# A hybrid diffusion step: the first feed-forward without Strassen products, squares summed by TensorE, and GpSimd kept off VectorE's work during normalisations

## The chip, the core and the metric

The kernel runs on one core of one Trainium2 chip. The metric is the device time of one execution in microseconds (us). Shown before the change: 2499.05 us, the median of 3 runs (2495.54 to 2499.7).

The core's engines are named as in the profile: PE is TensorE (matrix products, into the banks of PSUM), PEld its loading of stationary operands, DVE is VectorE, ACT is ScalarE, POOL is GpSimd, and SP is SyncE, which starts the transfers. Each engine runs its own stream of instructions in order.

## The reference

One step of a two-layer model over 128 context tokens and 512 latent tokens of width 1024. Each layer is a half-step SwiGLU feed-forward (FFN), a token mixer, and a second FFN. Layer 0 mixes by two attentions side by side (A, grouped-query with a band, and B, multi-head latent attention), layer 1 by a two-dimensional Fourier transform.

```python
def post_norm(x, out, gate, g, b):
    return layer_norm(ALPHA * x + gate[:, None, :] * out, g, b)
...
def half_ffn(x, shift, scale, gate, w_gate, w_up, w_down, g, b):
    h = modulate(x, shift, scale)
    return post_norm(x, FFN_HALF * swiglu(h, w_gate, w_up, w_down), gate, g, b)
...
    for l in range(DEPTH):
        mc = ada_mods(c_ctx[None, :], w_ada[l], b_ada[l])
        ms = ada_mods(c, w_ada[l], b_ada[l])
...
        y_s = half_ffn(y_s, ms[0], ms[1], ms[2], *ffn_pre)
        h_p = modulate(y_p, mc[3], mc[4])
...
        y_s = post_norm(y_s, o_s, ms[5], ln_g[l, 1], ln_b[l, 1])
...
        y_s = half_ffn(y_s, ms[6], ms[7], ms[8], *ffn_post)
```

All arithmetic is float32, and `modulate` is x * (1 + scale) + shift. The nine modulations of each layer (numbers 0 to 8: shift, scale and gate, three times) are matrix-vector products with a 1024 x 9216 matrix.

## The kernel before, in words

**Layout.** Features lie on the 128 partitions (eight tiles of them, `KT`), tokens along the free dimension. The 640 tokens are split in two halves, 256 and 384 columns at first and 254 and 386 later, so that one half's normalisation can run while TensorE works on the other half.

**Products.** A float32 product is made of three products of a high and a low part (`mm3`: hi*hi, hi*lo, lo*hi), so each weight and each activation is split first: a cast gives the high part (`hh`, `hd`, `wu`, `w`), a subtraction the low part (`hl`, and again `hd`, `wu`, `w`).

**The feed-forwards.** `ffn` lists units and runs them in order. The hidden width of 2816 is 22 blocks `f`. A "gk" unit (a head) and a "g" unit make the gate and up products of a block for one half, plain: 96 matmuls for a block, 48 on each half's columns. An "s" unit makes both for all tokens by a Strassen form: seven products of half-size operands, 84 matmuls of 320 columns for a block. Its operands are sums and differences of quarters of the activations (`form`, tiles `tmp` and `xt`, once for an FFN) and of the weights (`weights`, once for a block), and its seven results are added up by further VectorE instructions. `seven=(6, 17)` says which blocks are "s" units. The down products ("d" units) run by groups of blocks: `THREES` has eight groups, `FOURS` has six. Each "d" output is added to the residual `ya` with the gate (`ya<-a,gate,ya`). The first group's down products are called D0 below.

**The modulations.** `matvec` is one VectorE instruction over 128x1024 (it writes the tile `junk`, two instructions for each 512 KB load of `w_ada`). `ffn` spreads `ada` such loads over its length, the first `urgent` of them early. `ada_beside(16)` spawns 16 more beside the attention mixer.

**Normalisation.** `norm_sum` adds the eight tiles of `ya` as they come; `norm` has TensorE turn that sum into a mean on all partitions, subtracts it (`centre`), squares (`square`), adds the eight squares up in one tile `lns`, and calls `rstd`: a one-column matmul for each 128 columns (`psc<-ones,lns`) sums over the partitions, small VectorE instructions make the inverse root, and a matmul with a diagonal (`psc<-dg,ones`) brings it to all partitions. `apply` scales, and `h_split` makes the operands of the next products. The half that the next stage needs first is the held half (`self.hold`). A path with `delta`, used after the Fourier mixer and at the very end, sums squares another way.

**Who does what, in what order.** The class `Step` writes the program as a planner: each task is a generator, and it names the engines that could do its next instruction with an estimated duration for each. `choose` takes the engine that would start and end it first by the modelled clock; between VectorE ("v") and GpSimd ("g") that is

```python
        e = min(on, key=lambda e: max(now, starts[e]) + on[e] + SPARED * (e == "v"))
```

so that an addition goes to GpSimd when VectorE's modelled queue is long. The order on each engine is fixed by this when the program is built.

Of the kernel before, what the change touches and what calls it, by code (L numbers as in the profile page):

```python
# [19 lines left out]
D = 1024  # L20
# [262 lines left out]
class Step:  # L283
# [7 lines left out]
    def __init__(self, ctx, tc, io):  # L291
# [9 lines left out]
        self.side, self.begun, self.hold, self.order = [], 0, 0, ORDER  # L301
        self.const = self.pool(ctx, "const")
# [90 lines left out]
    def choose(self, on, what):  # L393
# [6 lines left out]
        now = self.nc.tensor.t if self.clock.fixed > 100 else 0  # L400
        e = min(on, key=lambda e: max(now, starts[e]) + on[e] + SPARED * (e == "v"))
# [165 lines left out]
    def rstd(self, q, n, eps, out, delta=None, banks=None):  # L567
# [4 lines left out]
        width = q.shape[1]  # L572
        k = -(-width // 128)
        if delta is None:
            yield "t", q
        yield "t", lambda: banks.free(1) and self.smalls.free(1) and self.diags.free(1)
        col, t, dg = banks.take(), self.smalls.take(), self.diags.take()[:, :width]
        v, hv, y = t[:, 0, :k], t[:, 1, :k], t[:, 4, :k]

        cs = [min(i * 128, width - 128) for i in range(k)]  # L580
# [14 lines left out]
        for i, c in enumerate(cs):  # L595
            self.mm(col[:, i:i + 1], q[:, c:c + 128], self.ones[:, 0:1], start=True, stop=True)
        self.sums.give(q)
# [147 lines left out]
    def square(self, half, st, o, n):  # L745

        ya = self.ya[half]
        if o:
            yield None, lambda: self.tmps.free(1)
        eng = yield {"s": 93 + 0.833 * n, **sums(n)}, ya[o]  # L750
        if o:
            yield None, lambda: self.tmps.free(1)
        sq = self.tmps.take()[:, :n] if o else st["q"]
# [4 lines left out]
        if o == 5 and "d" not in st:  # L758
# [12 lines left out]
    def norm(self, half, st, i, aff, ag, plain=False, spill=None, kept=True):  # L771
# [4 lines left out]
        self.hold += held  # L776
        delta = st.get("d")
# [8 lines left out]
        if delta is None:  # L786
            self.sums.give(s)
            yield "v", lambda: self.sums.free(1)
            st.update(q=self.sums.take()[:, :n], squares=0)
# [15 lines left out]
        q = st["q"]  # L805
# [6 lines left out]
        yield from self.rstd(q, D, LN_EPS, bc, delta, banks)  # L812
# [12 lines left out]
        def apply(o):  # L825
# [3 lines left out]
            if not left[0]:  # L829
                banks.give(bc)  # L830
                self.hold -= held
            if aff is None:
# [32 lines left out]
    def start(self, ops):  # L865
# [6 lines left out]
        raws, owner = {}, {}  # L872

        def load(o):
            for m in (1, 0):

                sl = owner[o, m] = self.xt if len(raws) % 2 else ops
                raws[o, m] = sl.take(dtype=F32)[:, :D]
# [18 lines left out]
        def weighed(o):  # L897
# [4 lines left out]
            owner[o, 1].give(raws[o, 1])  # L902
            known[o] += 1

        def scale(o):
# [5 lines left out]
            owner[o, 1].give(raws[o, 1])  # L911
# [5 lines left out]
        def shift(o):  # L917
# [3 lines left out]
            owner[o, 0].give(raws[o, 0])  # L921
            known[o] += 1

        def part(half, o):
# [4 lines left out]
            yield None, lambda: self.xroom(o)  # L929
            eng = yield scaled(self.n[half], len(self.segs[half])), sh  # L930
            yield None, lambda: self.xroom(o)
            t = self.xplace(half, o)
            self.modulated(eng, half, z, (s1, sh), o, t)
            self.spawn(alpha(z), "g", z)
            yield from self.h_split(half, o, t, self.h, False)
# [1664 lines left out]
```

## Time and profile before

| | |
|---|---|
| median of 3 runs | 2499.05 us |
| the profiled execution's own time | 2503.09 us |
| its span, first to last instruction | 2501.3 us |
| mean granted TensorE clock | 0.961 |
| PE busy | 2356.0 us (94%), 15113 instructions |
| DVE busy | 2011.3 us (80%), 4099 |
| ACT busy | 948.5 us (38%), 2071 |
| POOL busy | 574.2 us (23%), 557 |
| read from HBM | 247.79 MB, 101 GB/s over the span |

The profiled execution is one single run, and rows of the trace belong to it. Its span runs from the first to the last instruction; the 1.8 us between span and time lie around it. Busy time is the time in which an engine had an instruction under way. The granted clock is the share of full speed that TensorE was given, 1.00 being 2.4 GHz and 0.50 being 1.2 GHz.

The stages, by the tiles that the trace names: first FFN to 510 us, attention mixer to 880, its output product and normalisation to 930, second FFN of layer 0 to 1398, first FFN of layer 1 to 1880, Fourier mixer to 2036, last FFN to 2478, last normalisation to the end.

### The profile page before, as it was taken

The page shows a single profiled execution, that of the slowest core. Times are in us where ns is not written, and L with a number is a line of the kernel's source. Part 1 is how long each engine was busy: PE and PEld are TensorE (multiplying, and loading weights), DVE is VectorE, ACT ScalarE, POOL GpSimd, SP SyncE. Part 2 cuts the span into 40 slices and gives each one's busy share as a digit, 9 for nine tenths or more (in the row PEclk, how much of TensorE's full clock was granted, in tenths as well). Part 3 has the DMA queues.
Part 4 walks back from the last instruction along what each step waited for, and adds up shares of the span by engine and source line. Part 5 has one row for each costly group of instructions (what it writes and reads, how often), then busy time and mean ns, then how long its engine had stood idle before and what let it go on. Part 6 is the DMA issues. An engine that isn't in the chain of part 4 may idle for free. (4 is left out here: it accounts for less than half of the span.)

```text
span 2501.3 us, 40294 instructions
## 1 busy us (share of the span) xinstructions
PE 2356.0 (94%) x15113; PEld 2248.9 (90%) x15113; DVE 2011.3 (80%) x4099; ACT 948.5 (38%) x2071; POOL 574.2 (23%) x557
## 2 busy tenths in 40 slices
PE   7999999989989998999999899999996999999996
PEld 6999999978568898999999889999995788999996
DVE  7868999689667778688995887989969798777766
ACT  3323442253556634233331432434225344444332
POOL 7301011052322333011110530002116452000001
PEclk7999999999799998999999899999998999999998
DMA  6433335233122212333352043434524211222211
GB/s 247 140 96 115 119 127 196 91 109 96 30 63 66 78 62 81 118 118 122 124 167 87 18 131 97 127 127 132 164 86 153 93 51 44 88 88 86 85 60 43
DMA packets 98562, 258.02 MB, mean 103 GB/s; under 512 B 15224, under 2 KB 28216, under 8 KB 98368
## 3 DMA queue, kind: packets, MB, share of 16 engines
q1 hardware_dynamic: 98368, 255.45, 31.7%
q8 instruction: 119, 1.95, 0.3%
q14 instruction: 75, 0.61, 0.1%
HBM read 247.79 MB, written 5.52 MB: 101 GB/s over the span
## 5 line engine op out<-in xcount | busy, mean ns | idle before, releaser
L463 PE MATMUL a<-hh,wu 128*128 128x254 f32 (+4 forms) x2856 | 689.2, 315 | 13.4 <-POOL wu L200 7.8
L463 PEld LDWEIGHTS a<-hh,wu 128*128 128x128 f32 x2856 | 501.4, 192 | 15.7 <-POOL wu L200 8.1
L463 PE MATMUL a<-hd,wu 128*128 128x386 f32 (+3 forms) x2736 | 460.4, 313 | 16.9 <-ACT tmp L200 5.8
L463 PEld LDWEIGHTS a<-hd,wu 128*128 128x128 f32 x2736 | 420.2, 192 | 20.5 <-ACT tmp L200 6.0
L463 PE MATMUL a<-hl,wu 128*128 128x320 f32 (+4 forms) x1356 | 426.0, 314 | 8.6 <-POOL hl L200 7.7
L200 ACT CAST wu<-raw 128x512 fp32r<-128x512 f32 (+1 forms) x422 | 276.6, 676 | 398.3 <-DMA raw<-in_w_gu 126.8
L200 DVE CUSTOM_DVE_ANT_0 junk<-raw,cond,bada 128x1024 bf16<-128x1024 f32 x256 | 353.6, 1381 | 21.5 <-DMA raw<-in_w_ada 19.0
L200 DVE SCALAR_TENSOR_TENSOR ya<-a,gate,ya 128x128 f32<-128x128 f32 (+3 forms) x768 | 297.5, 433 | 70.7 <-PE a L463 67.7
L200 DVE TENSOR_TENSOR wu<-raw,wu 128x512 fp32r<-128x512 f32 (+1 forms) x362 | 285.2, 799 | 40.4 <-ACT wu L200 36.0
L463 PE MATMUL a<-hh,w 128*128 128x320 f32 (+6 forms) x1192 | 311.2, 317 | 2.1 <-ACT hh L200 2.1
L463 PE MATMUL a<-xt,wu 128*128 128x320 f32 (+2 forms) x1868 | 294.2, 310 | 4.2 <-ACT tmp L200 4.2
L463 PEld LDWEIGHTS a<-xt,wu 128*128 128x128 f32 x1868 | 277.5, 188 | 7.5 <-ACT tmp L200 5.9
L463 PEld LDWEIGHTS a<-hl,wu 128*128 128x128 f32 x1356 | 260.5, 192 | 10.9 <-POOL hl L200 8.5
L200 POOL TENSOR_TENSOR wu<-raw,wu 128x512 fp32r<-128x512 f32 (+1 forms) x57 | 97.1, 1708 | 584.6 <-ACT wu L200 511.7
L463 PE MATMUL a<-hd,w 128*128 128x386 f32 (+3 forms) x1200 | 223.3, 313 | 4.3 <-POOL hd L200 1.7
L463 PEld LDWEIGHTS a<-hh,w 128*128 128x128 f32 (+1 forms) x1192 | 212.6, 190 | 5.8 <-ACT hh L200 3.5
L463 PE MATMUL a<-hl,w 128*128 128x320 f32 (+6 forms) x668 | 211.1, 316 | 1.2 <-POOL hl L200 1.1
L463 PEld LDWEIGHTS a<-hd,w 128*128 128x128 f32 x1200 | 188.4, 190 | 6.6 <-POOL hd L200 2.2
L200 ACT CAST w<-raw 128x512 fp32r<-128x512 f32 (+3 forms) x189 | 122.6, 659 | 188.6 <-DVE raw L200 67.8
L200 ACT CAST hd<-tmp 128x320 fp32r<-128x320 f32 (+4 forms) x176 | 79.1, 459 | 227.3 <-DVE tmp L200 185.4
L200 POOL TENSOR_TENSOR w<-raw,w 128x512 fp32r<-128x512 f32 (+3 forms) x44 | 64.9, 1478 | 423.4 <-ACT w L200 382.0
L200 DVE TENSOR_TENSOR tmp<-tmp,a 128x320 f32<-128x320 f32 (+4 forms) x126 | 61.0, 484 | 95.9 <-PE a L463 89.2
(441 smaller groups left out, 3489.2 us busy)
## 6 DMA issues: line engine op xcount, KB each, us to landing
raw<-in_w_gu SPq DMA_DIRECT2D x176, 512.0 KB, 4.2
raw<-in_w_ada SPq DMA_DIRECT2D x128, 512.0 KB, 3.7
raw<-in_w_dn SPq DMA_DIRECT2D x176, 256.0 KB, 2.9
raw<-in_w_fin SPq DMA_DIRECT2D x16, 520.0 KB, 5.0
raw<-in_w_ab SPq DMA_DIRECT2D x11, 512.0 KB, 4.7
xt<-in_w_ada SPq DMA_DIRECT2D x8, 512.0 KB, 7.5
raw<-in_w_abo SPq DMA_DIRECT2D x8, 512.0 KB, 4.1
raw<-in_w_fout SPq DMA_DIRECT2D x8, 512.0 KB, 3.7
```

Source lines behind the costliest of these rows:

```text
L200: return getattr(self.engine, op)(*args, **kw)
L463: pe.engine.matmul(out, w, x, **kw)
```

## The change

Six things change:

1. The first FFN is plain throughout (`seven=None`), with the six groups of `FOURS`; it has 18 work slots where it had 10 and another pool beside them.
2. A counter `norming` is up while any normalisation runs. While it is up, `choose` doesn't give GpSimd anything that VectorE could do.
3. In the half that is not held, and without `delta`, each squared tile goes to TensorE, which sums it by one-column matmuls that accumulate in a bank (`st["col"]`), in place of additions into one tile.
4. The 16 loads and 32 matrix-vector instructions beside the attention mixer are gone. The first FFN has 8 loads more (48), the second 8 more, early ones (40, of them 8 urgent).
5. In the FFNs with no urgent modulations, D0 stood right behind the heads; now it stands behind the next plain or Strassen block, as in the first FFN.
6. Loads for the next stage, issued at an FFN's end, are no longer held back during a held half's normalisation.

```diff
+        if self.norming and "v" in on:
+            on = {e: on[e] for e in on if e != "g"}
         e = min(on, key=lambda e: max(now, starts[e]) + on[e] + SPARED * (e == "v"))
...
-        for i, c in enumerate(cs):
+        for i, c in enumerate(() if summed else cs):
             self.mm(col[:, i:i + 1], q[:, c:c + 128], self.ones[:, 0:1], start=True, stop=True)
...
+        if "col" in st:
+            yield "t", sq
+
+            for i, c in enumerate(cs := self.blocks(n)):
+                self.mm(st["col"][:, i:i + 1], sq[:, c:c + 128], self.ones[:, 0:1],
+                        start=not st["squares"] and not i, stop=st["squares"] == KT - 1 and i == len(cs) - 1)
+            self.tmps.give(sq)
+        elif o == 5 and "d" not in st:
...
+            if held:
+                yield "v", lambda: self.sums.free(1)
+                st.update(q=self.sums.take()[:, :n], squares=0)
+            else:
+
+                yield "t", lambda: banks.free(1)
+                st.update(col=banks.take(), squares=0)
...
-            if g == last or g == 1 and not urgent:
+            if g == last:
                 units, held = units + held, []
...
-                self.load_in(*e[2:4], 0 if e[4:] and e[4] < urgent else -1)
+                self.ada_live += e[4:] not in ((), (None,))
+                self.load_in(*e[2:4], 0 if e[4:] and (e[4] is None or e[4] < urgent) else -1)
...
-                ops = self.work_slots(pool, 10, True)
+                ops = self.work_slots(pool, 18, True)
...
-                self.ffn(0, 0, 0, (0, 3), pool, ops, {}, 0, THREES, 40, 8, after, True, spill=saved, kept=False)
+                self.ffn(0, 0, 0, (0, 3), pool, ops, {}, 0, FOURS, 48, 8, after, True, seven=None, spill=saved, kept=False)
...
-            self.spawn(self.ada_beside(16), first=-2)
...
-                self.ffn(0, 1, 2, (1, 0), pool, ops, old, 5, THREES, 32, 0, self.first_blocks(1, 0, got, ops, 2, is_w))
+                self.ffn(0, 1, 2, (1, 0), pool, ops, old, 5, THREES, 40, 8, self.first_blocks(1, 0, got, ops, 2, is_w))
```

Counted in the two programs: the first FFN loses 924 matmuls of 320 columns and gains 528 of 384 and 528 of 256. The summing of squares uses 42 one-column matmuls more (three normalisations with 16 in place of 2). GpSimd's stream falls from 545 to 452 instructions.

**Squares, between the FFNs of layers 0 and 1.** On TensorE, before the change, the squares of the 254-column half are one tile `lns` that two one-column matmuls sum (the other names are the products of the half that came first, with `hh` and `hl` its high and low parts):

```order
L463 MATMUL a_14634<-hh_85,w_14242 128x386
L463 MATMUL a_14635<-hh_85,w_14244 128x386
L463 MATMUL a_14635<-hl_93,w_14244 128x386
L463 MATMUL a_14635<-hh_85,w_14245 128x386
L463 MATMUL psc_14795<-ones,lns_14735 128x1 x2
L463 MATMUL a_14761<-hh_78,wu_14716 128x386
L463 MATMUL a_14761<-hl_86,wu_14716 128x386
```

With the change, at the same place, each squared tile `tmp` has its own pair; four pairs stand here, and the other four follow at once:

```order
L468 MATMUL a_14381<-hh_84,w_13995 128x386
L468 MATMUL psc_14467<-ones,tmp_14481 128x1 x2
L468 MATMUL psc_14467<-ones,tmp_14490 128x1 x2
L468 MATMUL a_14380<-hh_85,w_13991 128x386
L468 MATMUL a_14380<-hl_93,w_13991 128x386
L468 MATMUL a_14380<-hh_85,w_13992 128x386
L468 MATMUL a_14381<-hh_85,w_13994 128x386
L468 MATMUL a_14381<-hl_93,w_13994 128x386
L468 MATMUL a_14381<-hh_85,w_13995 128x386
L468 MATMUL psc_14467<-ones,tmp_14507 128x1 x2
L468 MATMUL psc_14467<-ones,tmp_14510 128x1 x2
```

The two matmuls with `lns` became eight pairs with `tmp`, spread between the products of the 386-column half; the squares come from ScalarE here, and no addition of squares is left.

**D0 in the first FFN of layer 1.** On TensorE, before the change, the last head's products (`hh_85` with `wu`) are followed at once by D0 (`hd`):

```order
L463 MATMUL a_15174<-hh_85,wu_14816 128x254
L463 MATMUL a_15174<-hl_93,wu_14816 128x254
L463 MATMUL a_15174<-hh_85,wu_14837 128x254
L463 MATMUL a_15249<-hd_14792,wu_14886 128x254
L463 MATMUL a_15249<-hd_14793,wu_14886 128x254
L463 MATMUL a_15249<-hd_14792,wu_14886 128x254
```

With the change another block's products follow the heads:

```order
L468 MATMUL a_14930<-hh_85,wu_14604 128x254
L468 MATMUL a_14930<-hl_93,wu_14604 128x254
L468 MATMUL a_14930<-hh_85,wu_14676 128x254
L468 MATMUL a_15005<-hh_78,wu_14724 128x386
L468 MATMUL a_15005<-hl_86,wu_14724 128x386
L468 MATMUL a_15005<-hh_78,wu_14738 128x386
```

and D0 comes 96 matmuls later, behind the last of that block:

```order
L468 MATMUL a_15102<-hh_85,w_14845 128x254
L468 MATMUL a_15102<-hl_93,w_14845 128x254
L468 MATMUL a_15102<-hh_85,w_14866 128x254
L468 MATMUL a_15134<-hd_14552,w_14870 128x254
L468 MATMUL a_15134<-hd_14553,w_14870 128x254
L468 MATMUL a_15134<-hd_14552,w_14870 128x254
```

Between the last head and D0 a whole block now stands, on both halves.

**GpSimd at the start of the second FFN of layer 0.** Before the change, the 386-column half's operands (`xt`, `hl`), a weight's low part (`wu`) and the residual's scaling (`ya`):

```order
L200 TENSOR_SCALAR xt_9630<-ya_0_9167,affa,affb 128x386
L200 TENSOR_SCALAR xt_9644<-ya_2_9169,affa,affb 128x386
L200 TENSOR_TENSOR hl_87<-xt_9630,hh_79 128x386
L200 TENSOR_SCALAR xt_9674<-ya_4_9171,affa,affb 128x386
L200 TENSOR_SCALAR xt_9674<-ya_5_9172,affa,affb 128x386
L200 TENSOR_TENSOR wu_10044<-raw_9835,wu_9837 128x1024
L200 TENSOR_SCALAR ya_1_9168<-ya_1_9168,ag 128x386
L200 TENSOR_SCALAR ya_4_9171<-ya_4_9171,ag 128x386
L200 TENSOR_TENSOR tmp_10038<-xt_9630 128x320
```

With the change, from the same half's normalisation on:

```order
L200 TENSOR_TENSOR lns_9286<-lns_9286,ya_4_8888 128x386
L200 TENSOR_TENSOR wu_9474<-raw_9332,wu_9473 128x1024
L200 TENSOR_TENSOR lns_9286<-lns_9286,ya_7_8891 128x386
L200 TENSOR_SCALAR ya_0_8884<-ya_0_8884,ag 128x386
L200 TENSOR_SCALAR ya_1_8885<-ya_1_8885,ag 128x386
L200 TENSOR_SCALAR ya_2_8886<-ya_2_8886,ag 128x386
L200 TENSOR_TENSOR tmp_9846<-xt_9347 128x320
```

The `xt` and `hl` instructions are gone from GpSimd's stream here. Its `wu` now stands between two additions of the sum for the mean (`lns<-lns,ya`), ahead of the normalisation.

## Rows read from the trace of the kernel before

**Rows 1.** Windows: us, busy (x count) per engine, PEclk, DMA share, GB/s.
```profile
20.00:68.00 48.00, 36.70 (x175) 35.43 (x176) 43.92 (x54) 15.81 (x35) 45.94 (x37) 0.71 0.52 193
104.00:131.50 27.50, 23.27 (x146) 22.64 (x145) 23.37 (x46) 5.94 (x9) 0.70 (x1) 0.94 0.48 147
131.50:487.00 355.50, 349.61 (x2339) 347.58 (x2338) 297.50 (x535) 116.91 (x224) 47.77 (x34) 1.00 0.40 127
560.00:625.00 65.00, 62.36 (x390) 57.74 (x389) 60.94 (x139) 22.88 (x50) 15.19 (x11) 0.95 0.31 94
625.00:810.00 185.00, 171.78 (x859) 124.54 (x858) 134.20 (x413) 107.97 (x334) 54.95 (x95) 0.89 0.19 54
880.00:975.00 95.00, 83.21 (x521) 81.69 (x520) 77.17 (x165) 37.48 (x77) 37.49 (x38) 0.91 0.12 40
1398.00:1450.00 52.00, 43.83 (x245) 42.34 (x246) 44.99 (x85) 26.46 (x56) 36.92 (x36) 0.87 0.11 32
1450.00:1480.00 30.00, 24.21 (x151) 23.42 (x150) 26.00 (x46) 10.29 (x20) 8.60 (x7) 0.83 0.51 152
2150.00:2200.00 50.00, 50.00 (x341) 50.00 (x340) 37.65 (x71) 20.90 (x42) 4.29 (x3) 1.00 0.30 95
```

**Rows 2.** Timeline of PE: start, us, engine, instruction; first and last of nine.
```profile
446.46 0.34 PE L463 MATMUL a<-hl,wu 128*128 128x384 f32 x1
...
447.87 0.34 PE L463 MATMUL a<-hh,wu 128*128 128x384 f32 x1
```

**Rows 3.** Timeline of PE, 578 us: six matmuls from the first start to the last.
```profile
578.07 0.40 PE L463 MATMUL a<-hh,wi 128*128 128x256 f32 x2
...
578.79 0.40 PE L463 MATMUL a<-hh,wi 128*128 128x256 f32 x2
```

**Rows 4.** Groups by tile junk: ns min/median/max, first to last start.
```profile
L200 DVE CUSTOM_DVE_ANT_0 junk<-raw,cond,bada x256: 1268/1282/2387, 90.3 to 1830.3; 128x1024 bf16<-128x1024 f32 x128
L200 DVE CUSTOM_DVE_ANT_0 junk<-xt,cond,bada x16: 1285/1761/1902, 8.6 to 62.8; 128x1024 bf16<-128x1024 f32 x16
```

**Rows 5.** Groups on POOL, 20 to 68 us: busy us, mean ns.
```profile
L200 POOL TENSOR_TENSOR xt<-tmp,xt 128x320 fp32r<-128x320 f32 x8 | 13.1, 1648 | 0.6 <-ACT xt L200 0.6
```

**Rows 6.** Waits of PE, 0 to 130 us: total, times, longest.
```profile
PE a L463 <- POOL hl L200: 7.7, 3, 3.0
```

**Rows 7.** Timeline of DVE, 573 to 583 us.
```profile
573.24 1.28 DVE L200 CUSTOM_DVE_ANT_0 junk<-raw,cond,bada 128x1024 bf16<-128x1024 f32 x1
...
582.77 1.22 DVE L200 TENSOR_TENSOR lns<-lns,tmp 128x384 f32<-128x384 f32 x2
```

**Rows 8.** Waits of PE, 575 to 592 us.
```profile
PE psc L463 <- DVE lns L200: 2.6, 1, 2.6
```

**Rows 9.** Timeline of POOL at 948 us.
```profile
948.46 2.69 POOL L200 TENSOR_TENSOR wu<-raw,wu 128x1024 fp32r<-128x1024 f32 x1
```

**Rows 10.** Waits of PE, 936 to 956 us.
```profile
PE a L463 <- POOL wu L200: 7.8, 1, 7.8
```

**Rows 11.** Timeline of DVE at 1413 us.
```profile
1413.18 2.55 DVE L200 TENSOR_TENSOR lns<-lns,tmp 128x254 f32<-128x254 f32 x1 [0.58 <-POOL lns L200]
```

**Rows 12.** Timeline of POOL at 1413 us.
```profile
1413.10 2.34 POOL L200 TENSOR_TENSOR wu<-raw,wu 128x1024 fp32r<-128x1024 f32 x1
```

**Rows 13.** Waits of PE, 1396 to 1425 us.
```profile
PE psc L463 <- POOL lns L200: 8.5, 2, 6.9
```

**Rows 14.** Waits of PE, 1455 to 1470 us.
```profile
PE a L463 <- ACT hd L200: 4.4, 1, 4.4
```

**Rows 15.** Timeline of PE at 592 us: one-column matmuls and the next one.
```profile
592.71 0.50 PE L463 MATMUL psc<-ones,lns 128*128 128x1 f32 x4
593.07 0.36 PE L463 MATMUL a<-hh,wi 128*128 128x256 f32 x1
```

**Rows 16.** Groups by tile lns, 2478 us to the end: ns min/median/max.
```profile
L200 POOL TENSOR_TENSOR lns<-lns,tmp x7: 717/723/789, 2480.3 to 2487.1; 128x254 f32<-128x254 f32 x7
```

**Rows 17.** Timeline of DVE at 2483 us.
```profile
2482.77 0.41 DVE L200 TENSOR_TENSOR lns<-lns,ya 128x254 f32<-128x254 f32 x1
```

More of the change, by code (lines that the diff above doesn't have):

```diff
@@ L594, in rstd @@
             yield "t", q
-        for i, c in enumerate(cs):
+        for i, c in enumerate(() if summed else cs):
             self.mm(col[:, i:i + 1], q[:, c:c + 128], self.ones[:, 0:1], start=True, stop=True)
-        self.sums.give(q)
+        if not summed:
+            self.sums.give(q)
         yield "v", col
@@ L928, in part @@
             yield "s", s1
-            yield None, lambda: self.xroom(o)
+            yield None, lambda: self.tmps.free(1)
             eng = yield scaled(self.n[half], len(self.segs[half])), sh
-            yield None, lambda: self.xroom(o)
-            t = self.xplace(half, o)
+            yield None, lambda: self.tmps.free(1)
+            t = self.tmps.take()[:, :self.n[half]]
             self.modulated(eng, half, z, (s1, sh), o, t)
             self.spawn(alpha(z), "g", z)
-            yield from self.h_split(half, o, t, self.h, False)
+            yield from self.h_split(half, o, t, self.h, True)
         def alpha(z):
@@ L944, in rest @@
                 if o + 1 < KT:
-                    yield None, lambda: self.begun >= min(o + 1, 4) and (o < 3 or known[o - 3] == 2) and self.xt.free(1 + sum(x is None for x in self.xs)) and ops.free(1)
+                    yield None, lambda: self.begun >= min(o + 1, 4) and (o < 3 or known[o - 3] == 2) and ops.free(2)
                     load(o + 1)
@@ L980, in ffn @@
         self.order = order
-        fast = lambda f: seven[0] <= f < seven[1]
+        fast = lambda f: seven and seven[0] <= f < seven[1]
+        xt = self.xt if seven else None
         last = len(groups) - 1
@@ L1027, in spare @@
         def spare(key, late):
-            return key[0] == "dn" and late and self.xt.free(5 if nxt else 1) and dnx[0] < (4 if nxt else 8)
+            return seven and key[0] == "dn" and late and self.xt.free(5 if nxt else 1) and dnx[0] < (4 if nxt else 8)
         def may(key, late):
@@ L1072, in back @@
             for t in ts:
-                (self.xt if t.tensor.name in self.xt.names else ops).give(t)
+                (xt if seven and t.tensor.name in xt.names else ops).give(t)
         def operand(key, src, dst, name, late=False):
@@ L1147, in ffn @@
             todo.append((5, 5, src, fn, a) if a < urgent else (t + 1, t, src, fn, a))
[L1148 removed]
+        todo += [(len(units) - 4, end_t, src, fn, None) for src, fn in after]
         todo.sort(key=lambda t: t[0])
@@ L1405, in ffn @@
         self.spawn(opened())
-        self.spawn(form(0), first=-1.5)
+        if seven:
+            self.spawn(form(0), first=-1.5)
         for t, u in enumerate(units):
```

54 lines of the change are left out of this document (27 added, 27 removed).

## The prediction

> **What bounds the kernel now.** I first read the windows, stage by stage, because the shares of the whole span mix stages with different limits. In the body of an FFN, TensorE never stops: in 50 us of the last FFN it is busy for 50.00, at a granted clock of 1.00, while VectorE is busy for 37.65 [rows 1]. There only fewer or shorter matmuls help. Between the stages it is otherwise. What such a place costs I reckon as the idle time plus the busy time times the missing clock, since a matmul at the lower of the two levels (1.2 in place of 2.4 GHz) takes longer without counting as idle. By rows 1: 20 to 68 us loses 48.0 - 36.7 = 11.3 idle and 36.7 x 0.29 = 10.6, in all 21.9; 104 to 131.5 loses 4.2 + 1.4 = 5.6; the body of the first FFN (131.5 to 487) 5.9; 560 to 625 loses 2.6 + 3.1 = 5.7; 625 to 810 loses 13.2 + 18.9 = 32.1; 880 to 975 loses 11.8 + 7.5 = 19.3; 1398 to 1450 loses 8.2 + 5.7 = 13.9; 1450 to 1480 loses 5.8 + 4.1 = 9.9. The engine that is full in these places is mostly VectorE: 43.9 of 48 us, 23.4 of 27.5, 60.9 of 65, 45.0 of 52, 26.0 of 30. In 20 to 68 us GpSimd is full as well (45.9). Then I read the waits of TensorE in each place, and the timelines of the engine it waits for.
>
> **The first FFN without Strassen: about +21.** 924 matmuls of 320 columns go. One takes 50.00/341 = 0.1466 us [rows 1], in all 135.5. In come 528 of 384 columns, at (447.87 - 446.46)/8 = 0.176 us [rows 2], and 528 of 256 columns, at (578.79 - 578.07)/6 = 0.120 us [rows 3]: 92.9 + 63.4 = 156.3. That is +20.8, certain to within 1 us, because this stage is bound by TensorE (349.6 of 355.5).
>
> **What that gives back.** In the body the 5.9 us of waits are partly for Strassen sums; I take -3 (bounds 0 and -5.9). At the start the forms of the activations disappear. On GpSimd the group `xt<-tmp,xt` alone is 13.1 us of its 45.9 [rows 1, 5], and the matvecs there run at 1.76 us in the median where later ones take 1.28 [rows 4]. TensorE waits 7.7 us there for `hl` from GpSimd [rows 6]. Of the 21.9 us lost I take -10. The floor is -4, half of the wait for `hl`: the DMA engines are busy to 0.52 on average at 193 GB/s [rows 1], so the loads may set the pace next. The other bound is -15, some two thirds of the loss. D0 follows the heads by 96 matmuls more than before, which is longer than the 5.6 us lost there: -5 (bounds 0 and -5.6). Here the modulation's matvecs for the gate are the thing that could be late again, as there are 8 more loads to be spread over the FFN; they are not early ones.
>
> **No matvecs beside the mixer: -9.** 32 instructions of 1.28 us [rows 4] leave VectorE's queue, 41 us in a stretch of 250 us. The clear case is at 583 us. There a run of matvecs starts at 573.24, and the sum of squares that TensorE needs comes behind them at 582.77 [rows 7]; TensorE waits 2.6 us for it [rows 8], and the clock of that stretch is 0.95. All 5.7 us of 560 to 625 hang on this place: -6. In 625 to 810 VectorE is busy for 134 of 185 us, so it has slack, and the 32.1 us lost are a chain of small steps through ScalarE, VectorE and TensorE. I take a tenth, -3. Bounds: -6 with nothing there, -25 with 60% of it (a rival below). The 16 loads come back in the two FFNs, 8 x 2 x 1.28 = 20 us more of VectorE in each, behind matmuls. The first FFN has room for it (297.5 of 355.5 us busy, less the Strassen sums). If the second had none, its share would be up to 20 us; the last FFN has 12 of 50 us free [rows 1], so I price it at +1, inside the "others" below.
>
> **GpSimd kept away, squares on TensorE: -14 in two places.** At 948 us the operands of the second FFN pass through GpSimd, and its `wu` takes 2.69 us [rows 9], behind which TensorE stands for 7.8 us [rows 10]. With the change `xt`, `hl` and this `wu` go to VectorE or ScalarE. I take the whole wait, -8, of the 19.3 lost (bounds -11, with the clock coming back earlier; +2, if VectorE, 77 of 95 us busy, takes up as much as is gained). At 1413 us VectorE's addition takes 2.55 us [rows 11] beside a `wu` of 2.34 on GpSimd [rows 12]; alone such an addition takes 0.41 [rows 17]. TensorE waits 6.9 us for the sum of these squares [rows 13]. With the change the eight squares go to TensorE as they come, and neither instruction is in the way. The last square still has to come behind the centring on VectorE, so I take -6 of the 13.9 (bounds -3 and -10).
>
> On that pair of rows the Trainium skill, page "SBUF — State Buffer", section "Who interferes with whom", says that a VectorE instruction with two SBUF inputs and a GpSimd instruction that reads SBUF share a read port, and that the one that issues later is fully blocked. The trace agrees here: 1413.10 + 2.34 = 1415.44 is when `wu` ends, and the addition ends at 1415.73. By that rule alone, moving an addition off GpSimd in the last normalisation would give VectorE more than it costs, and the sum would be some 4 us lower than mine.
>
> **D0 one block later in the first FFN of layer 1: -9.** Of the 9.9 us lost in 1450 to 1480 the wait is for `hd`, 4.4 us in one piece [rows 14], and the rest is clock. With a block of 96 matmuls in between (48 x 0.12 + 48 x 0.176 = 14 us) `hd` is ready. Bounds -6 and -9.9.
>
> **What it costs elsewhere.** One-column matmuls: four records take 593.07 - 592.71 = 0.36 us [rows 15], and one matmul makes two records, so 0.18 us each. 42 more are 7.6 us if none falls in a wait; I take +5 (bounds +3 and +7.6). The last normalisation: seven additions leave GpSimd, 0.72 us each [rows 16], for VectorE at 0.41 [rows 17], and VectorE sets the end there: 7 x 0.41 = 2.9, less a little contention, +2.5 (bounds -2, and 7 x 0.72 = +5). Others (D0 of the second and of the last FFN, the Fourier mixer, loads that are no longer held back): -3, from -8 to +3. The last FFN's D0 waits too, but there the Strassen operands come due in its place, so I count little.
>
> **The sum.** 20.8 - 3 - 10 - 5 - 9 - 14 - 9 + 5 + 2.5 - 3 = -24.7. Against the profiled execution, 2503.1 us, that is 2478.4. The median of the runs is 4 us (0.16%) below that execution, so I forecast 2474 us. About 0.2% (5 us) is what a measurement of this kernel can tell from no change.
>
> **The rivals.**
>
> *VectorE becomes the bound of the normalisations (slower).* GpSimd loses 93 instructions. Some 50 are Strassen forms and sums of the first FFN; the other 43 are moved. If all went to VectorE's chain at 0.41 to 0.61 us (a 384-column addition is 1.22/2 [rows 7]), that is 18 to 26 us, and the -14 above would not come: -24.7 + 14 + 22 = +11, so 2514 on the profiled execution, 2510 on the median. It decides where what is moved exceeds VectorE's free time, 7 us in 1398 to 1450 and 18 us in 880 to 975. Against it: ScalarE, busy for 26.5 of 52 and 37.5 of 95 us, takes the squares there, and much of what moves are additions that the squares on TensorE remove. Chance 0.08. The Trainium skill, page "Perfetto Trace Analysis", section "Optimizing Scalar/DVE Operations", speaks for this rival: when VectorE is saturated, offloading to ScalarE or even GpSimd may make sense, which is the opposite of this change; it adds that the port shared with GpSimd may undo that.
>
> *Only the price is sure (small gain).* The start is paced by loads (-4), the mixer only loses the wait at 583 us (-6), the Strassen waits stay as others (0), the one-column matmuls cost all of 7.6: +6 + 3 + 3 + 2.6 on the sum, -10, so 2493 and 2489 on the median. With one more term at its bound (880 to 975 us at 0) it is 2497, no change. For it: DMA at 0.52 at the start, and 50 us of slack of VectorE in 625 to 810. Chance 0.22, of which a third within 0.2%.
>
> *The mixer gains much (faster still).* If VectorE's in-order queue, not its total, sets the attention's steps, 60% of the 32.1 us come back, -19 in place of -3: 2462, on the median 2458. [...] Chance 0.18.
>
> The forecast itself, within 8 us, has 0.48; 0.04 remains for worse. **Chances:** faster by over 0.2% 0.82, within 0.2% 0.09, slower 0.09. The range of 8 in 10 goes from 2453, below the third rival, to 2494, above the second.
>
> **What would show it.** Right: the first FFN's body about 21 us longer with TensorE at 99%; 20 to 68 us with GpSimd far below 45 us; no matvec between 530 and 860 us; no wait for `wu` at the second FFN's start; no wait of 6.9 us, and `tmp` in place of `lns` in the one-column matmuls; no wait for `hd` behind the heads. Wrong: TensorE waiting for a DMA in the first 70 us; waits for VectorE (`hl`, `lns`, `dg`) as long as those for GpSimd were; TensorE stopping at one-column matmuls one square after another, eight short waits for one long one; VectorE at 95% or more around the normalisations.

## The result and the profile after

The change takes 2474.78 us, the median of 4 runs (2472.74 to 2478.62), beside 2499.38 us before: a ratio of 0.9903, with a 95% interval of 0.9888 to 0.9918. In a later comparison the same program gave 2470.80 us and a ratio of 0.9875 (0.9857 to 0.9892). It is faster by 1.0 to 1.3%. The profiled execution has a span of 2471.0 us.

The head of the page after (busy us, share of the span, instructions):

```profile
span 2471.0 us, 40363 instructions
PE 2362.2 (96%) x15329; PEld 2258.7 (91%) x15329; DVE 1910.5 (77%) x3928; ACT 917.6 (37%) x2000; POOL 499.0 (20%) x462
```

VectorE lost 101 us of busy time and GpSimd 75, while TensorE gained 6: it does more, in a shorter span. The windows after, at the same places as [rows 1] (from 533 us on they start 24 to 27 us earlier than there, as the stages do):

```profile
20.00:68.00 48.00, 43.80 (x260) 42.19 (x261) 44.80 (x66) 18.76 (x37) 28.10 (x21) 0.89 0.58 217
104.00:131.50 27.50, 27.50 (x191) 27.50 (x190) 18.58 (x36) 4.62 (x6) 0.00 (x0) 1.00 0.45 142
131.50:487.00 355.50, 355.43 (x2405) 354.80 (x2404) 239.79 (x419) 83.07 (x143) 9.90 (x6) 1.00 0.41 129
533.00:598.00 65.00, 63.21 (x422) 57.74 (x421) 50.77 (x118) 27.51 (x58) 19.39 (x12) 1.00 0.21 65
601.00:786.00 185.00, 169.12 (x862) 122.72 (x862) 111.82 (x372) 110.10 (x344) 53.60 (x95) 0.91 0.13 36
856.00:951.00 95.00, 88.87 (x562) 85.77 (x561) 72.27 (x159) 38.17 (x77) 39.36 (x36) 1.00 0.14 45
951.00:1001.00 50.00, 44.55 (x280) 43.72 (x279) 46.56 (x75) 13.99 (x25) 19.22 (x12) 0.97 0.50 158
1373.00:1425.00 52.00, 49.55 (x303) 48.56 (x303) 43.78 (x94) 32.66 (x68) 23.91 (x26) 0.90 0.13 36
1425.00:1455.00 30.00, 30.00 (x216) 29.99 (x215) 27.45 (x49) 12.38 (x25) 5.37 (x5) 1.00 0.54 172
```

By idle time plus busy time at the missing clock, 20 to 68 us now loses 4.2 + 4.8 = 9.0 in place of 21.9, D0 and the body of the first FFN nothing, the mixer's entry 1.8 in place of 5.7, the second FFN's start (856 to 951) 6.1 in place of 19.3, the place between the FFNs (1373 to 1425) 2.5 + 5.0 = 7.4 in place of 13.9, D0 of the first FFN of layer 1 (the third FFN below) nothing in place of 9.9. The attention itself loses as much as before (15.9 + 15.2 = 31.1, before 32.1). One row has no counterpart among those before: 951 to 1001 us, in the second FFN, idles for 5.5 us, with VectorE at 46.6 of 50. Before, the same stretch lost nothing:

```profile
975.00:1025.00 50.00, 50.00 (x323) 49.98 (x323) 38.63 (x69) 13.37 (x21) 1.04 (x1) 1.00 0.42 134
```

Longer stages can be timed against marks that every version has, the first `psc<-dg,ones` of a normalisation (the first and the last FFN end with their last down product). The table gives the length of each stage in us, in one profiled execution of each kernel; the experiments are named as below. "Entry" is the first FFN's normalisations, the mixer's first products and two small normalisations within the mixer.

| kernel | first FFN | entry | attention, output | second FFN | to the next FFN | third FFN | Fourier mixer | last FFN | end |
|---|---|---|---|---|---|---|---|---|---|
| before | 509.4 | 107.3 | 285.6 | 491.1 | 33.4 | 447.7 | 163.5 | 440.5 | 22.9 |
| the change | 502.2 | 87.6 | 288.6 | 495.2 | 28.2 | 442.7 | 157.1 | 442.8 | 26.6 |
| after_again | 502.8 | 87.8 | 285.8 | 494.1 | 27.2 | 441.9 | 160.9 | 442.4 | 26.6 |
| plain_only | 501.1 | 104.8 | 288.0 | 488.4 | 32.0 | 449.3 | 165.0 | 442.4 | 22.9 |
| strassen_first | 519.5 | 93.9 | 288.4 | 493.9 | 27.2 | 442.1 | 158.4 | 442.1 | 26.6 |
| strassen_first_ada | 510.4 | 103.3 | 291.4 | 484.6 | 28.2 | 442.2 | 165.7 | 442.2 | 26.6 |
| ada_back | 503.2 | 98.7 | 283.1 | 485.3 | 27.2 | 441.5 | 159.4 | 442.2 | 26.6 |
| no_norming | 502.9 | 91.2 | 287.6 | 502.2 | 25.9 | 449.9 | 170.0 | 439.3 | 22.9 |
| no_col | 503.0 | 89.8 | 284.9 | 494.9 | 27.3 | 453.2 | 167.7 | 442.9 | 26.6 |
| d0_early | 502.6 | 87.6 | 286.4 | 493.9 | 27.2 | 451.8 | 166.0 | 439.5 | 26.6 |
| d0_last | 502.3 | 87.6 | 288.5 | 495.2 | 28.4 | 442.5 | 170.6 | 440.5 | 26.6 |
| loads_held | 502.7 | 87.6 | 286.5 | 493.8 | 27.2 | 439.0 | 165.5 | 443.3 | 26.6 |
| tail_free | 503.1 | 87.6 | 289.9 | 493.7 | 27.1 | 442.5 | 159.9 | 443.2 | 22.9 |
| combined | 502.8 | 98.7 | 286.1 | 484.7 | 25.6 | 441.5 | 158.3 | 440.3 | 22.9 |

after_again is the same program as the change, and d0_last and tail_free are the same up to the last FFN. So the table shows how far a stage differs between executions of one program: 285.8 to 289.9 in the attention, 157.1 to 170.6 in the Fourier mixer, about 1 to 2 elsewhere. Differences smaller than that say nothing. A mark also tells only when one instruction ran, not how much TensorE had done by then: where an edit changes the order, a loss can show in the next column.

### The profile page after: what moved, and what is told of

It is laid out like the page before. It is cut to its first block, busy times and chain, and to the rows that moved or that the text cites. A ratio compares the mean times of both kernels' runs of the same rounds, so it can differ in the third digit from the quotient of the medians.

```text
span 2471.0 us, 40363 instructions
## 1 busy us (share of the span) xinstructions
PE 2362.2 (96%) x15329; PEld 2258.7 (91%) x15329; DVE 1910.5 (77%) x3928; ACT 917.6 (37%) x2000; POOL 499.0 (20%) x462
## 4 chain that ended last, share of the span: by engine, by line
PE 78%; DVE 10%; DMA 4%; issue 3%; ACT 3%; POOL 2%; SPq 0%; DVEq 0%; ACTq 0%; POOLq 0%
PE a L468 69%; PE psc L468 3%; PE s L468 3%; DVE junk L200 2%; DVE ya L200 2%; DVE tmp L200 1%; DVE wu L200 1%; PE ss L468 1%; DVE rs L200 1%; PE s L473 1%; DMA raw<-in_w_ada 1%; DMA wu<-in_w_ada 1%; DMA raw<-in_w_dn 1%; POOL ya L200 1%; DMA raw<-in_w_gu 1%
## 5 line engine op out<-in xcount | busy, mean ns | idle before, releaser
L468 PE MATMUL a<-hh,wu 128*128 128x254 f32 (+4 forms) x3344 | 784.6, 312 | 2.5 <-ACT hh L200 1.9
L468 PEld LDWEIGHTS a<-hh,wu 128*128 128x128 f32 x3344 | 577.6, 190 | 4.9 <-ACT hh L200 3.1
L468 PE MATMUL a<-hl,wu 128*128 128x254 f32 (+4 forms) x1592 | 496.3, 312 | 5.3 <-DVE hl L200 5.0
L200 DVE CUSTOM_DVE_ANT_0 junk<-raw,cond,bada 128x1024 bf16<-128x1024 f32 x256 | 357.6, 1397 | 18.8 <-DMA raw<-in_w_ada 15.9
L200 DVE SCALAR_TENSOR_TENSOR ya<-a,gate,ya 128x128 f32<-128x128 f32 (+2 forms) x720 | 279.2, 431 | 76.3 <-PE a L468 74.3
L468 PEld LDWEIGHTS a<-hl,wu 128*128 128x128 f32 x1592 | 302.4, 190 | 8.2 <-DVE hl L200 7.6
L468 PE MATMUL a<-hh,w 128*128 128x254 f32 (+6 forms) x1144 | 297.1, 315 | 6.5 <-ACT hh L200 6.5
L468 PE MATMUL a<-xt,wu 128*128 128x320 f32 (+2 forms) x1508 | 241.4, 313 | 15.0 <-ACT tmp L200 12.0
L468 PEld LDWEIGHTS a<-xt,wu 128*128 128x128 f32 x1508 | 226.7, 191 | 19.5 <-ACT tmp L200 14.6
L468 PE MATMUL a<-hl,w 128*128 128x254 f32 (+5 forms) x652 | 204.6, 314 | 1.6 <-DVE hl L200 1.4
L200 ACT CAST w<-raw 128x512 fp32r<-128x512 f32 (+3 forms) x166 | 110.0, 671 | 156.4 <-DVE raw L200 43.1
```

Source lines behind the costliest of these rows:

```text
L200: return getattr(self.engine, op)(*args, **kw)
L468: pe.engine.matmul(out, w, x, **kw)
```

## The experiments

The medians: each kernel against the kernel before, run beside it on the same chip.

| kernel | median us (runs) | ratio to before, 95% |
|---|---|---|
| plain_only | 2493.65 (12) | 0.9970 (0.9956 to 0.9984) |
| strassen_first | 2495.73 (12) | 0.9984 (0.9970 to 0.9997) |
| strassen_first_ada | 2491.91 (8) | 0.9957 (0.9941 to 0.9973) |
| ada_back | 2472.23 (4) | 0.9883 (0.9860 to 0.9906) |
| no_norming | 2486.76 (7) | 0.9950 (0.9933 to 0.9968) |
| no_col | 2495.19 (12) | 0.9973 (0.9962 to 0.9984) |
| d0_early | 2481.80 (6) | 0.9923 (0.9908 to 0.9939) |
| d0_last | 2467.72 (6) | 0.9874 (0.9852 to 0.9897) |
| loads_held | 2473.93 (5) | 0.9896 (0.9882 to 0.9910) |
| after_again | 2470.80 (4) | 0.9875 (0.9857 to 0.9892) |
| tail_free | 2472.27 (4) | 0.9878 (0.9858 to 0.9897) |
| combined | 2465.08 (4) | 0.9853 (0.9834 to 0.9872) |

**The plain first FFN: plain_only, strassen_first, strassen_first_ada.** plain_only is the kernel before with this part alone:

```diff
...
-                ops = self.work_slots(pool, 10, True)
+                ops = self.work_slots(pool, 18, True)
...
-                self.ffn(0, 0, 0, (0, 3), pool, ops, {}, 0, THREES, 40, 8, after, True, spill=saved, kept=False)
+                self.ffn(0, 0, 0, (0, 3), pool, ops, {}, 0, FOURS, 40, 8, after, True, seven=None, spill=saved, kept=False)
```

> The kernel before with the first part of the change alone: first FFN plain, six groups, 18 slots, the new start; matvecs stay beside the mixer (40 loads in the first FFN), GpSimd unrestricted, squares summed as before. Theory: the first FFN pays for its 20.8 us by itself, with 13 us at the start, 6 at D0 and 7 of Strassen waits, so its last down product ends some 7 us earlier than before (at about 502 us in place of 509.4) and the time is 2492 us (2488 to 2496). Rival: what came back there needs GpSimd restricted and the matvecs spread as well; then the last down product ends at 515 us or later and the time is 2505 us or more.

Its first FFN ends at 501.1 us, and the median is 2493.65: the theory holds, the longer matmuls are paid for in the stage itself.

strassen_first is the change without this part: the old start and slots, and the first FFN's call is

```diff
-                self.ffn(0, 0, 0, (0, 3), pool, ops, {}, 0, FOURS, 48, 8, after, True, seven=None, spill=saved, kept=False)
+                self.ffn(0, 0, 0, (0, 3), pool, ops, {}, 0, THREES, 48, 8, after, True, spill=saved, kept=False)
```

> The change without its first part: the first FFN keeps its Strassen blocks, eight groups and the old start, all else is changed (48 loads in the first FFN). Theory: the plain first FFN is worth 7 us, so this one takes 2482 us (2478 to 2486). Rival: the 20.8 us of plain matmuls are a net loss once the rest is changed; then it takes 2470 us or less.

Neither: 2495.73. The first FFN became longer than before, 519.5 us. Its body, 131.5 to 487 us, and a wait there:

```profile
131.50:487.00 355.50, 346.06 (x2306) 343.84 (x2305) 311.50 (x556) 119.12 (x226) 53.23 (x35) 0.99 0.44 138
PE a L468 <- ACT hd L200: 4.6, 2, 4.4
```

VectorE is busy for 311.5 us, where it was for 297.5 before [rows 1] and is for 239.8 in the change. So strassen_first_ada tells the 8 extra loads apart: the same, with 40 loads there and the matvecs beside the mixer (and, as in ada_back below, 32 loads in the second FFN).

```diff
-                self.ffn(0, 0, 0, (0, 3), pool, ops, {}, 0, THREES, 48, 8, after, True, spill=saved, kept=False)
+                self.ffn(0, 0, 0, (0, 3), pool, ops, {}, 0, THREES, 40, 8, after, True, spill=saved, kept=False)
...
+            self.spawn(self.ada_beside(16), first=-2)
```

> The kernel before with GpSimd's restriction, the squares on TensorE, the late D0 and the loads' priority, but with the Strassen first FFN and the matvecs where they were. Theory: the plain first FFN costs or gains by itself only what plain_only showed, 6 to 8 us, and the 20 us that strassen_first lost came from its 8 extra loads beside Strassen sums: 2480 us (2476 to 2484), first FFN's last down product at 509 to 511 us. Rival: the plain first FFN is worth 20 us whatever the loads: 2492 us or more, and the last down product at 517 us or later.

The place came out as the theory had it, 510.4 us: with Strassen sums 8 loads cost 9 us, with the plain FFN nothing (plain_only and ada_back have 40 loads, the change 48, and all end at 501 to 503). The time came out as the rival had it, 2491.91, some 20 us over ada_back, from which it differs by the first FFN alone. Of that the stages of the profiles show 7.2 in the first FFN and 4.6 in the entry. The entry's part can be seen. A sum of squares `lns` stands on VectorE behind a run of the mixer's matvecs, and TensorE waits longer for it. It also waits 2.1 us for another sum on GpSimd, for which ada_back doesn't wait. The waits for VectorE's sum from the first FFN's end on, in strassen_first_ada and then in ada_back:

```profile
PE psc L468 <- DVE lns L200: 6.5, 1, 6.5
```

```profile
PE psc L468 <- DVE lns L200: 2.7, 1, 2.7
```

Right behind the first FFN an `hl` on VectorE takes 2.35 us beside a `wi` of 2.37 on GpSimd. That is not the difference: the waits for `hl` come to 2.3 us in both kernels.

```profile
511.01 2.35 DVE L200 TENSOR_TENSOR hl<-tmp,hh 128x384 fp32r<-128x384 f32 x1
```

```profile
510.59 2.37 POOL L200 TENSOR_TENSOR wi<-raw,wi 128x1024 fp32r<-128x1024 f32 x1 [2.56 <-DVE ya L200]
```

The profiles differ by 27.5 us, and nearly all that is left of it lies in the attention (291.4 to 283.1) and the Fourier mixer (165.7 to 159.4), which vary between executions by nearly as much. The windows of these two stages, for strassen_first_ada and then for ada_back:

```profile
613.80:905.10 291.30, 273.65 (x1550) 215.03 (x1551) 210.88 (x618) 157.24 (x463) 78.68 (x120) 0.93 0.22 63
1860.10:2025.80 165.70, 150.45 (x837) 125.15 (x838) 133.83 (x367) 67.45 (x190) 81.31 (x74) 0.89 0.26 86
```

```profile
601.80:884.90 283.10, 266.15 (x1551) 211.87 (x1552) 209.37 (x616) 157.17 (x463) 78.30 (x120) 0.96 0.22 64
1838.80:1998.30 159.50, 143.60 (x838) 120.88 (x838) 134.92 (x367) 67.11 (x190) 80.98 (x74) 0.94 0.27 90
```

The instructions are the same in number and the idle time is nearly the same (17.7 and 15.3 us, against 17.0 and 15.9); the granted clock is lower. Over the whole execution, the first FFN included, it is lower in every run: 0.962 to 0.967 in the 8 of strassen_first_ada, 0.970 to 0.974 in the 4 of ada_back. That the first FFN sets the clock of these later stages is not shown.

**The matvecs beside the mixer: ada_back.** The change with them put back:

```diff
...
-                self.ffn(0, 0, 0, (0, 3), pool, ops, {}, 0, FOURS, 48, 8, after, True, seven=None, spill=saved, kept=False)
+                self.ffn(0, 0, 0, (0, 3), pool, ops, {}, 0, FOURS, 40, 8, after, True, seven=None, spill=saved, kept=False)
+            self.spawn(self.ada_beside(16), first=-2)
...
-                self.ffn(0, 1, 2, (1, 0), pool, ops, old, 5, THREES, 40, 8, self.first_blocks(1, 0, got, ops, 2, is_w))
+                self.ffn(0, 1, 2, (1, 0), pool, ops, old, 5, THREES, 32, 0, self.first_blocks(1, 0, got, ops, 2, is_w))
```

> The change with the 16 loads and 32 matvecs back beside the mixer (40 loads in the first FFN, 32 and none urgent in the second). Theory: most of the 17 us that the way from the first FFN's end to the attention gained come from these matvecs: 10 to 14 us come back between 510 and 625 us, the second FFN gains 2 to 6 for having 8 loads fewer, time 2483 us (2479 to 2488). Rival: that gain is from GpSimd's restriction and the squares on TensorE; then 510 to 625 us is as with the change to within 3 us, and the time is 2471 to 2475 us.

The time is the rival's, 2472.23, but not for the rival's reason. The entry takes 98.7 us in place of 87.6, as the theory had it; the second FFN takes 485.3 in place of 495.2, and gives the 11 us back. There the change has 16 matvecs from 948 to 978 us, early because the gate's modulation is now made in this FFN, which also needs it; ada_back has half as many, later. The groups by tile junk from 902 to 1000 us (ns min/median/max, first to last start), for the change and then for ada_back:

```profile
L200 DVE CUSTOM_DVE_ANT_0 junk<-raw,cond,bada x16: 1272/1286/2312, 948.2 to 977.9; 128x1024 bf16<-128x1024 f32 x16
```

```profile
L200 DVE CUSTOM_DVE_ANT_0 junk<-raw,cond,bada x8: 1275/1282/1796, 963.4 to 995.2; 128x1024 bf16<-128x1024 f32 x8
```

The 50 us behind the heads in ada_back, beside the row 951 to 1001 us above, and a wait of the change there:

```profile
957.00:1007.00 50.00, 50.00 (x328) 49.98 (x327) 38.66 (x69) 13.70 (x24) 8.56 (x6) 1.00 0.43 134
```

```profile
PE a L468 <- ACT tmp L200: 3.6, 1, 3.6
```

With the matvecs VectorE is at 46.6 of 50 us, D0 waits for ScalarE's `tmp<-a`, which comes late, and TensorE idles; without them it is busy for all 50. Moving the matvecs out of the mixer was worth 11 us there and cost 10 in the second FFN.

**GpSimd's restriction: no_norming and tail_free.**

```diff
-        if self.norming and "v" in on:
+        if False and "v" in on:
```

> The change without the restriction of GpSimd during normalisations. Theory: GpSimd was in the way; TensorE's waits for GpSimd's low parts and weights come back at the second FFN's start and behind the mixer's entry, the last normalisation gains up to 4 us, time 2480 us (2476 to 2485). Rival: in the second FFN's start and at the end the restriction only moved the wait to VectorE and ScalarE; then the time is 2466 to 2473 us, and the second FFN's start is 4 us shorter or more.

2486.76: undoing the restriction costs 12 to 16 us, more than expected. The second FFN is 7 to 8 us longer, the third 7 to 8, the Fourier mixer 9 to 13 (of which executions of one program may make as much), the entry 3.6; the end is shorter by 3.7. The waits that the theory named don't come back at the second FFN's start: from 880 to 960 us TensorE waits for GpSimd for 2.4 us in all, and not for a `wu`. What makes that FFN longer is mostly D0, where the change already loses 4.9 us behind the early matvecs: the two longest of the following waits (882 to 1384 us), 6.7 and 4.5 us, stand there.

```profile
PE a L468 <- ACT tmp L200: 15.6, 4, 6.7
```

The largest wait stands at the third FFN's start. It isn't for GpSimd but for a `wu` on VectorE:

```profile
PE a L468 <- DVE wu L200: 8.5, 1, 8.5
```

```profile
1423.20 1.88 DVE L200 TENSOR_TENSOR wu<-raw,wu 128x1024 fp32r<-128x1024 f32 x1
```

It runs beside Strassen sums on GpSimd; the same split takes 1.22 us at 1408.42 us, where GpSimd does nothing. But most of the wait is over when it begins: TensorE has stood since 1416.6. It comes late because the half's scaling and splits (`xt`, `hl`, `ya`) stand ahead of it on VectorE, some of them slow as well (an `hl` takes 0.97 us at 1421.30 and 0.62 at 1422.66).

tail_free lifts the restriction at the end only:

```diff
-        self.norming += 1
+        self.norming += aff is not None
...
-                self.norming -= 1
+                self.norming -= aff is not None
```

> The change with GpSimd allowed again in the last normalisation alone. Theory: the restriction costs 3.7 us there, so 2471 us (2468 to 2473), and the last 26.6 us are 22.9 again. Rival: the additions on GpSimd slow VectorE's by as much as they take off it: 2474 us, the end stays at 26 us.

The end takes 22.9 us again, as the theory had it, and the median doesn't show it: 2472.27 beside 2470.80 of the same program without the edit. The 4 runs of each spread over 3 to 5 us. The windows of the end, from the last FFN's last product on, for the change and for tail_free (the third busy time is VectorE's, the fifth GpSimd's):

```profile
2444.40:2471.00 26.60, 4.72 (x14) 3.32 (x14) 21.06 (x67) 10.12 (x20) 0.56 (x1) 0.55 0.28 99
```

```profile
2447.00:2469.80 22.80, 4.03 (x12) 3.02 (x12) 17.66 (x55) 9.43 (x18) 9.48 (x14) 0.55 0.33 115
```

9 us of GpSimd become 3.4 us of VectorE, and the end grows by those: here sharing the work is faster.

**The squares on TensorE: no_col.**

```diff
-            if held:
+            if True:
                 yield "v", lambda: self.sums.free(1)
```

> The change with the squares of the half that is not held summed in a tile again, and one one-column matmul for each 128 columns. Theory: the sums on TensorE are worth 5 us between the FFNs of layers 0 and 1 and little elsewhere, against 3 to 5 us of one-column matmuls: 2478 us (2474 to 2482), the wait in front of the one-column matmuls at 3 us or more in that place. Rival: with GpSimd out of the way the sum in a tile is as early, and the matmuls are pure cost: 2468 to 2472 us.

2495.19, neither: without them most of the change's gain is gone. The stage between the FFNs is no longer (27.3 us), but less is done in it. TensorE waits there for the sum and for what follows from it, where the change has neither wait:

```profile
PE psc L468 <- DVE lns L200: 4.9, 1, 4.9
PE psc L468 <- DVE dg L200: 4.8, 1, 4.8
```

```profile
1372.00:1424.00 52.00, 37.43 (x184) 34.37 (x184) 45.63 (x103) 31.22 (x65) 20.30 (x21) 0.84 0.12 36
```

These 52 us lose 14.6 + 6.0 = 20.6 us, where the change loses 7.4 from 1373 to 1425. The work left over falls into the third FFN, as part of the 10 us that it takes more. The second place is the entry to the Fourier mixer, whose stage is 7 to 11 us longer than in three of the four profiles of the change's program:

```profile
PE psc L468 <- DVE lns L200: 14.2, 1, 14.2
```

```profile
1864.42 3.35 DVE L200 TENSOR_TENSOR lns<-lns,tmp 128x254 f32<-128x254 f32 x3
...
1869.00 1.41 DVE L200 TENSOR_TENSOR lns<-lns,tmp 128x254 f32<-128x254 f32 x1
...
1875.85 0.41 DVE L200 TENSOR_TENSOR lns<-lns,tmp 128x254 f32<-128x254 f32 x1
```

The one-column matmul waits for a chain of VectorE additions that begins at 1864 and ends at 1876 us, each taking up to 1.4 us beside GpSimd's splits of the mixer's weights, and other work of VectorE's stands between them. In the change at the same place the one-column matmuls wait for ScalarE's squares, for 1.3 us:

```profile
PE psc L468 <- ACT tmp L200: 1.3, 2, 1.0
```

**The place of D0: d0_early and d0_last.**

```diff
-            if g == last:
+            if g == last or g == 1 and not urgent:
```

> The change with D0 behind the heads again in the FFNs without urgent modulations, which are the first and the last of layer 1. Theory: the first of layer 1 loses its 10 us (a wait for hd of some 4 us comes back), the last gains 3, time 2482 us (2479 to 2485). Rival: the wait for hd came from GpSimd's place in the split of hd, which is changed anyway; then 2473 to 2476 us.

As the theory had it: 2481.80. The wait for `hd` behind the heads is back, the third FFN takes 451.8 us in place of 442, and the last one 439.5 in place of 442.5.

```profile
PE a L468 <- ACT hd L200: 5.3, 1, 5.3
```

d0_last has D0 early in the last FFN only (`g == 1 and (l, j) == (1, 1)`).

> The change with D0 behind the heads in the last FFN alone. Theory: there a block behind the heads needs the Strassen operands earlier than they are ready (8 us of short waits), so D0 early gives back 3 us: 2472 us (2469 to 2475). Rival: the operands are late either way, or D0 waits as it did before (5.9 us): 2474 to 2479 us.

The last FFN takes 440.5 us in place of 442.8, as expected. The median is 2467.72 us, a little under the theory's range; the ratio, 0.9874, is not told apart from after_again's 0.9875.

**The loads' priority: loads_held.**

```diff
-                self.load_in(*e[2:4], 0 if e[4:] and (e[4] is None or e[4] < urgent) else -1)
+                self.load_in(*e[2:4], 0 if e[4:] and e[4] is not None and e[4] < urgent else -1)
```

> The change with the loads for the next stage at low priority again, so held back during a held half's normalisation. Theory: the 4.6 us that TensorE waits for a sum on GpSimd ahead of the Fourier mixer come from the splits of the mixer's weights, which GpSimd takes up earlier; held back, the wait shrinks under 2 us and the time is 2471 us (2468 to 2474). Rival: the weights come too late then, and the start of the mixer loses 8 us as before the change: 2478 us or more.

2473.93 lies in the theory's range, but is no change that these runs can tell, and the theory's mechanism fails: the wait for GpSimd's sum is not shorter, 5.6 us in place of 4.4. So it doesn't hang on this priority. The third FFN ends 3 us sooner, but its normalisation then waits 7.3 us for `dg`, which the Fourier mixer's stage holds (165.5 us):

```profile
PE psc L468 <- DVE dg L200: 7.3, 1, 7.3
PE psc L468 <- POOL lns L200: 5.6, 1, 5.6
```

**All that helped, together: after_again and combined.** The reference is the change as it is:

> The change as it is, as the reference for the three others on the same chip: 2474 us (2471 to 2478). The granted clock within the Fourier mixer is the one thing that may differ between its executions; if it falls there as in one other profile (0.86 in place of 0.98 at the same waits), the time is 8 to 12 us longer.

2470.80. combined has ada_back's edit, d0_last's and tail_free's.

> The change with the matvecs back beside the mixer, D0 early in the last FFN, and GpSimd allowed in the last normalisation. Theory: the three gains add up, 2.5 to 4 and 2.4 and 3.7 us: 2466 us (2462 to 2469). Rival: they overlap or fall to the clock of the Fourier mixer: 2470 us or more.

2465.08, as the theory had it, and the fastest kernel here, with the second FFN at 484.7 us, the last at 440.3 and the end at 22.9. It is faster than the kernel before by 1.5%. Than the change it is 5.7 us faster by the medians, of 4 runs each, and the intervals of the two ratios overlap a little.

## Why the prediction was right, and where its steps were not

The time, 2474.78, lies 0.8 us from the forecast of 2474. That it came so close is partly luck: terms were off on both sides, two of them by 9 to 10 us. Point by point, measured on the profiled executions, which differ by 30.3 us where the sum had 24.7 (the medians differ by 24.6):

- *The first FFN.* Forecast +20.8 - 3 - 10 - 5 = +2.8, measured -7.2 (509.4 to 502.2), and plain_only shows -8.3 from this part alone. The mechanism is right and the sizes were too small: all 5.9 us of the Strassen waits went, not 3, and the start gave back 12.9, not 10. D0 gave all of its 5.6. Together that is 24.4, so by the stage's length the plain products cost some 17 us net; 20.8 was called certain to within 1. The loads did not set the pace at the start: DMA is busy to 0.58, and the waits of TensorE left between 20 and 130 us are for VectorE's `hl`.
- *The matvecs beside the mixer.* Forecast -9, of which -6 in the entry; the entry gained 11 by ada_back. It gained 19.7 in all, and for the other 8.6 the sum had no term of its own. But their place in the second FFN was priced at +1 and cost 10: **this step failed**. It took the room in another FFN's body as cover, and the 8 early loads don't fall in the body: they fall behind the normalisation, where VectorE is full. For the attention's own steps the forecast had -3; they lose 31.1 us where they lost 32.1, less than executions differ by.
- *GpSimd kept away in the second FFN, -8.* Measured +4.1, with the failed step inside; ada_back, without it, has -5.8. The wait for `wu` at this FFN's start is gone, as forecast. But that GpSimd's restriction removed it is not shown: only the kernel before and plain_only have this wait (7.8 and 7.9 us), and no_norming, with GpSimd unrestricted, doesn't. Which of the other parts suffices stays open. What the restriction is seen to be worth lies at D0 of this FFN and at the third FFN's start, where the sum had nothing for it.
- *Squares between the FFNs, -6.* Measured -6.5 by windows (13.9 to 7.4). The mechanism holds: in no_col the wait for the sum is back there, and the place loses 20.6. But the same sums matter ahead of the Fourier mixer as well, a wait of 14.2 us in no_col, and that was put under "others". no_col is some 20 us slower than the change, as much as strassen_first, and the prediction had -6 + 5 for it.
- *D0 of the third FFN, -9.* d0_early against the change: 9 to 10 us in that stage, 7 to 11 in the median, in which the last FFN gives 3 back.
- *One-column matmuls, +5.* No stage shows them by itself. Added up over all stages, TensorE's busy time less what the lower clock cost is some 6 us more in the change than in no_col (an estimate from the two traces), within the bounds.
- *The end, +2.5.* Measured +3.7.
- *The last FFN* was counted little; D0 late costs 2.3 us there.

The rivals: that only the price is sure was wrong, since the start and the Strassen waits gave back more than forecast. That VectorE becomes the bound of the normalisations holds at the end of the program and, by the early matvecs, in the second FFN, but not as a whole. That the attention gains much was wrong; 601 to 786 us lost as much as before. On the Trainium skill's rule of the shared port ("SBUF — State Buffer", "Who interferes with whom"), by which the sum would have been 4 us lower at the end: there the estimate drawn from it fails, the end became 3.7 us longer. For single pairs the trace agrees with the rule (`hl` 2.35 us beside `wi` 2.37, and it ends 0.4 us after `wi`).

The parts are not additive. Undoing one part of the change costs 7 to 21 us for four of them (strassen_first, no_norming, no_col and d0_early against 2474.78), in all some 60 us, where the whole gains 25 to 32. plain_only gives 6 us alone and strassen_first loses 21 to 25 without it. A reading that fits, though no run singles it out: each part removes one of several things that held VectorE up in the same places, and with any of them left a wait comes back there or elsewhere. Of the 27.5 us between the profiles of strassen_first_ada and ada_back 12 lie in the first two stages, and the rest goes with the lower clock in the attention and the Fourier mixer; why it is lower stays open.

## What to carry to other kernels

Products that save TensorE's columns by additions on VectorE were a loss in this first FFN, whose start had VectorE busy for 43.9 of 48 us; the later FFNs keep them, and no run tried them plain. Look at what else could go into the freed VectorE time. Before work is moved from a full stretch to "a body with room", look at where its deadline puts it: work that is needed early lands in the next full stretch. A sum that TensorE waits for was better made by TensorE here, tile by tile, than by a chain of additions that shares its queue with everything else. What each part is worth is only known when it has been undone alone, and then the waits have to be read as well: a stage between two marks can keep its length while its work slips into the next, and a part can pay in another place than the one it was made for.

## What was not expected of the hardware

The granted clock of the Fourier mixer differs between executions of the same instructions with nearly the same waits (5.1 us in the change and 5.4 in d0_last, from 1869 us on to the mixer's next normalisation). From 1914 to 1944 us TensorE is busy all but without a gap in the change and in d0_last (the same program there). The windows (us, busy of PE, PEld, DVE, ACT, POOL, PEclk, DMA share, GB/s) of the change, then of d0_last:

```profile
1914.00:1929.00 15.00, 15.00 (x88) 10.59 (x87) 8.63 (x20) 5.00 (x18) 4.34 (x4) 1.00 0.14 51
1929.00:1944.00 15.00, 14.80 (x110) 13.11 (x109) 14.76 (x46) 4.22 (x12) 5.83 (x7) 1.00 0.52 177
```

```profile
1914.60:1929.60 15.00, 15.00 (x65) 9.30 (x64) 5.93 (x19) 4.88 (x17) 2.52 (x4) 0.84 0.22 67
1929.60:1944.60 15.00, 15.00 (x72) 13.59 (x71) 9.53 (x20) 2.27 (x6) 5.02 (x4) 0.59 0.52 176
```

Here the clock fell while TensorE was busy throughout, to 0.59 over 15 us, near the lower level of 1.2 GHz; in the change's profile it stayed at 2.4. The stage took 170.6 us in place of 157.1, and that profiled run 2483.95 us, where d0_last's other runs took 2464.67 to 2469.34. A stage's length in one profile is therefore no measure of a change there. Why it fell in one execution and not in the other, no run shows.
